# Moving a store's issue and the wait for a free output tile within one pipelined unit of a softmax-mixture kernel

## The chip, the cores and the metric

The kernel runs on one core of one Trainium2 chip; the metric is device microseconds of that core. A run counts as slow when it lies over 1.5% above the fastest run of the same kernel; slow runs are left out of the ratios.

## The reference

```python
# float32: logits (batch 32, seq 128, heads 4, vocab 4096), prior (32, 128, 4)
prior_probs = softmax(prior, axis=-1)
softmax     = softmax(logits, axis=-1)
mixture     = sum over heads of prior_probs[..., None] * softmax   # (32, 128, 4096)
```

268 MB come in, 67 MB go out, and each number is touched a few times: there is little arithmetic per byte.

## The kernel before

The 4096 rows are worked off in 32 units (U = 32) of 128 rows. The helper `only` replaces all inferred waits of an instruction by the ones named. `H` is the number of heads, 4; `bufd` is true for all units but the last two. A unit's logits go to one of two input tiles, its result to one of two output tiles (`obuf`).

```python
def load(u):                       # issued by SyncE, 8.39 MB; cut finer for u = 0 and u >= 29
    ...
    only(ld, adds[u - 2, 0] ...)   # the input tile is free when add0 two units back is done
def store(u, acc, eng):            # 2.10 MB
    st = eng.dma_start(out=ov[u // J, u % J], in_=acc)         # shortened
    stores[u] = only(st, adds[u, H - 1])                       # waits for the unit's last add
...
def exp(h, *keep):                 # ScalarE, 4096 columns, sum of the row in dsum
    ex = nc.scalar.activation(es[h], lt[:, h], AF.Exp, accum_out=dsum[:, u, h : h + 1])
    keep = (loads[u, h],) + keep
    if bufd and h and u:
        keep += (adds[u - 1, h],)
    exps[u, h] = only(ex, *keep)
def weigh(h, n, *keep):            # 1 / sum on VectorE, times prior on GpSimd
    rc = nc.vector.reciprocal(rden[:, u, h : h + n], dsum[:, u, h : h + n])
    only(rc, exps[u, h + n - 1])
    mul = nc.gpsimd.tensor_mul(coeff..., rden..., ppu...)      # shortened
    return only(mul, rc, *keep)
...
free = (stores[u - 2],) if bufd and u >= 2 else ()   # the output tile's last store
m = H if u < U - 4 else 2                            # one group of four heads, two of two at the end
for h in range(H):
    late = h == H - 1 and 4 <= u < U - 3
    if h == H - 1 and 0 < u < U - 3:
        store(u - 1, obuf[:, (u - 1) % 2], nc.scalar)          # issued by ScalarE
    exp(h, *((stores[u - 4],) if late else ()))
    if (h + 1) % m:
        continue
    g = h + 1 - m
    mul = weigh(g, m, *(free if g == 0 else ()))
    ...                                                        # add0 to add3 on VectorE
if u + 2 < U:
    load(u + 2)
```

I call the four exponentials of a unit exp0 to exp3 and its four multiply-adds add0 to add3. The output tile is first written by add0, which waits for the coefficient; so the wait for the tile may sit anywhere ahead of that.

The softmax here doesn't subtract the row's maximum and nothing guards it: scores larger than these inputs give would overflow.

## Time and profile before

| | kernel before |
|---|---|
| time, median of 6 runs | 780.94 us (780.90 to 781.00) |
| period of a unit in the middle | 24.17 us |
| load, issue to landing | 30.9 us |
| store, issue to landing | 29.4 us |
| ScalarE's wait for loads, sum | 280.6 us |

Most lines are shown in the prediction. Two more views help. The first is the page's chain of work that ended last, as shares of the span by engine:

```profile
DMA 64%; ACT 27%; DVE 6%; issue 2%; POOL 0%; DVEq 0%; POOLq 0%
```

Followed back from the end, most of the time is waiting for transfers. The second is the table of stretches; its columns are the stretch, its length, busy time of VectorE, ScalarE and GpSimd (with instructions), the clock, the share of time in which transfer engines are busy, and GB/s:

```profile
301.75:398.45 96.70, 63.94 (x21) 58.02 (x32) 0.80 (x4) 1.00 1.00 434
398.45:495.15 96.70, 63.94 (x21) 58.02 (x32) 0.81 (x4) 1.00 1.00 434
```

A stretch is four units. VectorE works 64 of 96.7 us, the transfers all of it.

### The profile page before, as it was taken

Reading aid. Unit: us, or ns where it says so; the run is one execution under the profiler, and the core shown is the slowest. Engines: PE = TensorE matmul, PEld = TensorE weight load, DVE = VectorE, ACT = ScalarE, POOL = GpSimd, SP = SyncE. Lnnn points to the kernel's source line nnn. Section 1 sums busy time; section 2 is a strip of 40 time slices with the busy share of each in tenths; the row PEclk is TensorE's granted clock in tenths of the full one; section 3 lists DMA queues with packets and bytes.
Section 4 is the critical chain, followed back from the end, with each engine's and each line's share of the span. In section 5 each row is a group of like instructions: output and inputs, shape, how many; then the busy total and the mean of one; then the engine's idle time right before and its main releaser. Section 6 shows DMA issues by size and latency. Waiting matters only on the chain.

```text
span 779.3 us, 654 instructions
## 1 busy us (share of the span) xinstructions
DVE 521.0 (67%) x174; ACT 466.7 (60%) x258; POOL 8.3 (1%) x41
## 2 busy tenths in 40 slices
DVE  4447875558755587555775557855578655689886
ACT  4476555775457755577555675546765567657782
POOL 0000000000000000000000000000000000000000
DMA  9999999999999999999999999999999999999998
GB/s 407 457 417 401 470 407 434 428 461 428 405 467 403 458 420 433 442 443 418 431 454 407 454 408 467 420 415 447 432 442 417 463 399 463 410 427 433 434 429 377
DMA packets 10117, 335.66 MB, mean 431 GB/s; under 512 B 1136, under 2 KB 1136, under 8 KB 1152
## 3 DMA queue, kind: packets, MB, share of 16 engines
q1 hardware_dynamic: 6048, 276.83, 82.3%
q10 hardware_dynamic: 4064, 58.79, 17.6%
q14 instruction: 5, 0.04, 0.0%
HBM read 268.50 MB, written 67.11 MB: 431 GB/s over the span
## 4 chain that ended last, share of the span: by engine, by line
DMA 64%; ACT 27%; DVE 6%; issue 2%; POOL 0%; DVEq 0%; POOLq 0%
DMA ltile<-in_logits_dram 62%; ACT ebuf L159 19%; ACT ltile L159 8%; DVE obuf L177 5%; DMA out_dram<-obuf 2%; DVE ltile L183 1%; POOL coeff L170 0%; DVE rden L168 0%; DVEq L240 0%; POOLq L240 0%; POOLq L170 0%
## 5 line engine op out<-in xcount | busy, mean ns | idle before, releaser
L183 DVE SCALAR_TENSOR_TENSOR obuf<-ebuf,coeff,obuf 128x4096 f32<-128x4096 f32 x90 | 403.6, 4484 | 3.8 <-POOL coeff L170 0.6
L159 ACT ACTIVATE ebuf<-ltile 128x4096 f32<-128x4096 f32 x90 | 322.9, 3589 | 7.4 <-DMA ltile<-in_logits_dram 7.4
L159 ACT ACTIVATE ltile<-ltile 128x4096 f32<-128x4096 f32 x38 | 137.3, 3614 | 280.6 <-DMA ltile<-in_logits_dram 280.6
L168 DVE RECIPROCAL rden<-dsum 128x4 f32<-128x4 f32 (+1 forms) x36 | 6.3, 175 | 227.9 <-ACT ebuf L159 225.1
L177 DVE TENSOR_SCALAR obuf<-ltile,coeff 128x4096 f32<-128x4096 f32 x30 | 70.6, 2353 | 10.2 <-POOL coeff L170 10.2
L183 DVE SCALAR_TENSOR_TENSOR ltile<-ltile,coeff 128x4096 f32<-128x4096 f32 (+1 forms) x7 | 27.0, 3875 | 0.8 <-POOL coeff L170 0.6
L159 ACT ACTIVATION_READ_ACCUMULATOR ebuf<-ltile 128x1 f32 x90 | 16.8, 186 | 0.0
L170 POOL TENSOR_TENSOR coeff<-rden,pp 128x4 f32<-128x4 f32 (+1 forms) x36 | 7.2, 200 | 755.3 <-DVE rden L168 745.4
L159 ACT ACTIVATION_READ_ACCUMULATOR ltile<-ltile 128x1 f32 x38 | 7.1, 186 | 0.0
L139 DVE TENSOR_REDUCE pmax<-pr 16x256 f32<-16x1024 f32 x1 | 1.2, 1208 | 7.8 <-DMA pr<-in_prior_dram 7.8
L141 ACT ACTIVATE pr<-pr 16x1024 f32<-16x1024 f32 x1 | 1.1, 1055 | 7.8 <-DVE pr L140 7.8
L177 DVE TENSOR_SCALAR ltile<-ltile,coeff 128x4096 f32<-128x4096 f32 x2 | 4.7, 2354 | 0.6 <-POOL coeff L170 0.6
L144 DVE TENSOR_TENSOR pn<-pr,pmax 16x1024 f32<-16x1024 f32 x1 | 1.9, 1939 | 0.1
L141 ACT ACT_TABLE_LOAD x1 | 1.3, 1283 | 1.2 <-PEq L229 1.2
L142 DVE TENSOR_REDUCE pmax<-pr 16x256 f32<-16x1024 f32 x1 | 1.2, 1207 | 1.1 <-ACT pr L141 1.1
L149 DVE STREAM_TRANSPOSE pp<-pn 32x256 f32<-32x256 f32 x4 | 1.7, 435 | 0.1
L143 DVE RECIPROCAL pmax<-pmax 16x256 f32<-16x256 f32 x1 | 1.7, 1741 | 0.0
L140 DVE TENSOR_TENSOR pr<-pr,pmax 16x1024 f32<-16x1024 f32 x1 | 1.2, 1211 | 0.0
L138 POOL MEMSET pn<- 32x1024 f32 x1 | 0.9, 941 | 0.3 <-POOLq L229 0.3
L229 POOL MEMSET const-bfloat16-1.0<- 128x1 bf16 x1 | 0.1, 106 | 0.0
L229 POOL MEMSET const-uint8-127<- 128x1 uint8 x1 | 0.1, 106 | 0.0
L229 POOL MEMSET const-float32-0.0<- 128x1 f32 x1 | 0.1, 103 | 0.2 <-issue 0.2
(1 smaller groups left out, 0.1 us busy)
## 6 DMA issues: line engine op xcount, KB each, us to landing
out_dram<-obuf ACTq DMA_DIRECT2D x28, 2048.0 KB, 29.4
ltile<-in_logits_dram SPq DMA_DIRECT2D x7, 4096.0 KB, 26.1
ltile<-in_logits_dram SPq DMA_DIRECT2D x2, 2048.0 KB, 30.9
out_dram<-obuf SPq DMA_DIRECT2D x2, 2048.0 KB, 33.9
out_dram<-ltile SPq DMA_DIRECT2D x1, 2048.0 KB, 17.2
out_dram<-ltile SPq DMA_DIRECT2D x2, 1024.0 KB, 4.8
ltile<-in_logits_dram SPq DMA_DIRECT2D x28, 30.9
pr<-in_prior_dram ACTq DMA_DIRECT2D x1, 64.0 KB, 7.0
```

Source lines behind the costliest of these rows:

```text
L139: nc.vector.reduce_max(pmax, pr, axis=AX.X)
L140: nc.vector.tensor_sub(pr, pr, pmax.unsqueeze(2).to_broadcast([G, R, H]))
L141: nc.scalar.activation(pr, pr, AF.Exp)
L142: nc.vector.reduce_sum(pmax, pr, axis=AX.X)
L143: nc.vector.reciprocal(pmax, pmax)
L144: nc.vector.tensor_mul(pn[0:G].rearrange("g h r -> g r h"), pr, pmax.unsqueeze(2).to_broadcast([G, R, H]))
L149: nc.vector.transpose(pp[32 * t : 32 * (t + 1)], pq[:, :, :, 32 * t : 32 * (t + 1)])
L159: ex = nc.scalar.activation(es[h], lt[:, h], AF.Exp, accum_out=dsum[:, u, h : h + 1])
L168: rc = nc.vector.reciprocal(rden[:, u, h : h + n], dsum[:, u, h : h + n])
L170: mul = nc.gpsimd.tensor_mul(coeff[:, u, h : h + n], rden[:, u, h : h + n], ppu[:, h : h + n])
L177: st = nc.vector.tensor_scalar(out=acc[:, lo:hi], in0=es[h][:, lo:hi], scalar1=coeff[:, u, h : h + 1], scalar2=None, op0=ALU.mult,)
L183: st = nc.vector.scalar_tensor_tensor(out=acc[:, lo:hi], in0=es[h][:, lo:hi], scalar=coeff[:, u, h : h + 1], in1=acc[:, lo:hi], op0=ALU.mu ...
```

## The change

The intent: get the store out sooner, and take the wait for the output tile off the short path from the last exponential to the first add, onto an engine that waits for loads anyway.

```diff
             for h in range(H):
-                late = h == H - 1 and 4 <= u < U - 3
-                if h == H - 1 and 0 < u < U - 3:
+                if h == 2 and 0 < u < U - 3:
                     store(u - 1, obuf[:, (u - 1) % 2], nc.scalar)
-                exp(h, *((stores[u - 4],) if late else ()))
+                exp(h, *(free if m == H and h == H - 1 else ()))
                 if (h + 1) % m:
                     continue
                 g = h + 1 - m
-                mul = weigh(g, m, *(free if g == 0 else ()))
+                mul = weigh(g, m, *(free if m < H and g == 0 else ()))
```

## The prediction

> **What bounds the kernel now.** I read the page first, then the transfer view of a steady stretch, then the waits, then the timeline of one unit. A unit is 128 rows: one 8.39 MB load, four exponentials (exp0 to exp3) on ScalarE, four multiply-adds (add0 to add3) on VectorE, one 2.10 MB store; there are 32. From the page:
>
> ```profile
> DVE 521.0 (67%) x174; ACT 466.7 (60%) x258; POOL 8.3 (1%) x41
> ...
> DMA  9999999999999999999999999999999999999998
> ...
> HBM read 268.50 MB, written 67.11 MB: 431 GB/s over the span
> ```
>
> No compute engine is above 67%, while the transfer engines are at 90% or more in 39 of 40 slices. Four units of the middle (400 to 496.7 us):
>
> ```profile
> DMA packets 1152, 41.94 MB, mean 434 GB/s; under 512 B 128, under 2 KB 128, under 8 KB 128
> ...
> q1 hardware_dynamic: 576, 33.55, 80.1%
> q10 hardware_dynamic: 576, 8.39, 20.3%
> ...
> out_dram<-obuf ACTq DMA_DIRECT2D x4, 2048.0 KB, 29.4
> ltile<-in_logits_dram SPq DMA_DIRECT2D x4, 30.9
> ```
>
> Loads (q1) and stores (q10) get the same number of packets, 576 each, and so bytes as 4 to 1, which is just what a unit needs. A load takes 30.9 us from issue to landing and a store 29.4, both longer than a unit's period of 24.17 us (96.7 / 4). So each queue gets its next transfer before its last has landed: neither runs dry. The rate table confirms it: six stretches of four units from 108 to 688 us all show 434 GB/s. Waits:
>
> ```profile
> POOL coeff L170 <- DVE rden L168: 745.4, 35, 28.3
> ACT ltile L159 <- DMA ltile<-in_logits_dram: 280.6, 32, 12.0
> ...
> POOL coeff L170 <- DMA out_dram<-obuf: 10.0, 1, 10.0
> ```
>
> ScalarE waits for loads in 32 units, 280.6 us in all. GpSimd, which today waits for the store two units back before the coefficient, is held by it once, in the tail; elsewhere it waits for VectorE's reciprocal. The wait that moves is free where it stands.
>
> **What the Trainium skill says.** "DMA: Bandwidth & Descriptors", section "Queues, rings and completion order": each transfer engine goes round-robin between its queues, a packet at a time. The 576 against 576 agree. The same page, section "Where 436 GB/s comes from", puts the fabric's ceiling at 435 GB/s; the 434 agrees. It also says that HBM at about 358 GB/s binds such transfers; this trace, one core alone, shows 434, and the measurement decides. "Perfetto Trace Analysis", section "Per-engine timelines": ScalarE's sequencer puts a compute instruction in a queue and goes on, but waits for a transfer's semaphores itself. Both show in unit 26:
>
> ```profile
> 645.09 3.62 ACT L159 ACTIVATE ltile<-ltile 128x4096 f32<-128x4096 f32 x1 [9.65 <-DMA ltile<-in_logits_dram]
> ...
> 648.71 3.60 ACT L159 ACTIVATE ebuf<-ltile 128x4096 f32<-128x4096 f32 x1
> 651.90 0.34 ACTq L113 DMA_DIRECT2D out_dram<-obuf  x1
> ...
> 652.31 3.56 ACT L159 ACTIVATE ebuf<-ltile 128x4096 f32<-128x4096 f32 x1
> ...
> 655.90 3.60 ACT L159 ACTIVATE ebuf<-ltile 128x4096 f32<-128x4096 f32 x1
> ...
> 659.63 0.18 DVE L168 RECIPROCAL rden<-dsum 128x4 f32<-128x4 f32 x1 [7.75 <-ACT ebuf L159]
> ...
> 662.51 4.48 DVE L183 SCALAR_TENSOR_TENSOR obuf<-ebuf,coeff,obuf 128x4096 f32<-128x4096 f32 x1
> ```
>
> The store's issue stands after exp2 in the program, yet goes out at 651.90, before exp2 starts at 652.31. What it waited for is add3 of the unit before, which ends at 638.35 + 13.53 = 651.88.
>
> **The change, part by part.** The order of VectorE's and SyncE's instructions and their waits is unchanged; ScalarE and GpSimd have as many instructions as before.
>
> 1. *The store's place.* 28 stores (0 to 27, each issued in the unit after its own) move one exponential forward. The gain is nothing: the issue is already held by add3 (0.02 us from 651.88 to 651.90), not by its place. The cost: exp2 now stands behind it. It can start at 651.88 + 0.02 + 0.34 (the issue) + 0.03. The last term is the gap at the start of the trace between the end of ScalarE's first transfer issue, 0.79 + 0.39 = 1.18, and the table load behind it at 1.21. That gives 652.27, against 652.31 today: in step by chance, no delay. This makes a new loop: add3, issue, exp2, exp3, reciprocal, coefficient, add0 to add3. From exp2's start to the end of add3 it is 662.51 + 13.52 - 652.31 = 23.72 us, and with the 0.39 it is 24.11, against the 24.17 at which the transfers let units through. If the gap is really 0.15, the loop is 24.23, and compute drifts back by 0.06 x 27 units = 1.6 us over the whole run.
>
> 2. *The wait.* GpSimd loses its wait for the store two units back in the four-wide units, 26 of its multiplications. exp3 trades its wait for the store four units back (from unit 4), long landed, for the store two units back. Store 24 goes out at 627.74 and takes 29.4, so it lands at 657.1; exp3 would start at 655.90 and now waits until 657.1, 1.2 us. GpSimd's multiplication at 659.88 found it landed. So a hidden wait becomes a visible one, in nearly every unit. It doesn't add up per unit, though: landings are 24.17 us apart, so exp3 is late by 1.2 us in every unit, once for all. Add3 then ends 676.03 - 655.90 = 20.13 us after the landing, and its store goes out 24.17 - 20.15 = 4.0 us before the store ahead of it lands. The store queue stays fed.
>
> 3. *What the delay does to loads.* The load two units ahead goes out when add0 ends. Today that is at 662.51, and the load in flight lands at 638.34 + 30.9 = 669.25: 6.7 us ahead. Later by 1.2 us it is 5.5 us ahead; with the drift of part 1 still 3.9. If the load queue did empty for a moment, the store queue would hold a store with over 13 us to go (it went out 10.6 us before the load's issue and needs 24 or more), and the engines would move that. Bytes only trade places; idle engines would need both queues empty at once.
>
> Sum for the steady part: 0 us, out of 1.2 to 2.8 us of later compute that lies beside transfers.
>
> 4. *Head and tail.* In unit 2, add3 of unit 1 ends at 59.15 + 13.53 = 72.68, later against the load than in the middle, so exp2 slips from 71.80 to about 73.1, and load 4 from 82.00 to 83.3, still 4.8 us before load 3 lands at 88.15. In the tail units 28 and 29 keep their wait on GpSimd, on stores 26 and 27. Store 27 goes out some 1.2 to 2.5 us later than 700.23, and the one visible GpSimd wait, which ends at 718.33, moves with it. That delays add0 and add1 of unit 29 (ending 725.53), but add2 starts only at 727.94, behind exp3 of that unit: up to 2.4 us are swallowed. Load 31's first part goes out with the end of that add0, at 721.03, and starts its first exponential at 749.22, with 28 us in between that are transfers queued ahead of it: hidden. Those bytes are the same, so the end stays, give or take half a microsecond.
>
> Predicted: 780.93 + 0 steady + about 0.1 for head and tail = 781.0 us.
>
> **The rivals.**
>
> *The new wait stalls ScalarE and is paid in each unit.* For it: exp3 visibly waits 1.2 us, and 1.2 x 26 = 31 us would make 812. Against: ScalarE is idle about 9.65 us in each unit before exp0, waiting for the load, and takes the 1.2 out of that; and landings keep a 24.17 us rhythm of their own.
>
> *The loop through the store's issue becomes the bound.* 24.11 is only 0.06 under the period. If the gap behind the issue is 0.5 us, the loop is 24.58, and in 27 units compute falls 0.41 x 27 = 11 us behind the loads. The first 5 are covered by the queue's lead, 6 come onto the time: 787 us. For a loss of 2% (15.6 us) the gap must be about (15.6 + 5) / 27 + 0.06 = 0.8 us; the one such gap in the trace is 0.03.
>
> *Earlier or better spaced stores help.* A stretch at 434 GB/s has nothing to give. All bytes at that rate take 335.6 MB / 434 = 773.3 us of 779.3; the 6 us of difference are the first transfer's start and the drain after the last add, which this doesn't touch. A gain of 2% is out of reach; at best the tail, at 420 GB/s over its last 91 us, gives 2 us: 779.
>
> **Range and chances.** The central case is no change; repeats of the kernel before lie within 0.1 us. Downward there are at most some 1.5 us of better mixing in the tail; upward the drift, up to about 3 us. Range 779.5 to 783.8. Faster by over 2%: 0.01; slower by over 2%: 0.03, nearly all of it the second rival; within 2%: 0.96.
>
> **What would show it.** Right: in the middle 434 GB/s, equal packets, period 24.17; a new wait of ScalarE for stores of 1 to 2 us in most units, its wait for loads smaller by as much; the store's issue again 0.02 us after add3, with exp2 right behind it; store latency down from 29.4 to about 28 us, and load latency from 30.9 to about 29.5; GpSimd's only wait for a store still in the tail. Wrong: a period above 24.2 with idle transfer slices (the loop bounds), a load landing late in unit 30 or 31, or a gap of over 0.5 us between the store's issue and exp2.

## The result, and the profile after

The changed kernel takes 780.98 us (median of 6 runs, 780.91 to 781.09), the kernel before 780.94 beside it. The ratio is 1.0001, with a 95% interval from 0.9988 to 1.0013. (A ratio is the mean time of one kernel's fast runs over that of the other's in the same rounds, so not quite the ratio of the medians.) The time is the same; the inside isn't. The transfers of four units in the middle (400 to 496.7 us) of the changed kernel:

```profile
DMA packets 1152, 41.94 MB, mean 434 GB/s; under 512 B 128, under 2 KB 128, under 8 KB 128
...
out_dram<-obuf ACTq DMA_DIRECT2D x4, 2048.0 KB, 28.0
ltile<-in_logits_dram SPq DMA_DIRECT2D x4, 29.5
```

The bytes and the rate are those of before. Both latencies are 1.4 us shorter: each transfer is issued later and lands when it did. Its waits (who for whom, sum in us, times, longest):

```profile
ACT ltile L159 <- DMA ltile<-in_logits_dram: 241.5, 32, 12.0
...
ACT ebuf L159 <- DVE obuf L183: 36.0, 26, 2.1
...
POOL coeff L170 <- DMA out_dram<-obuf: 10.7, 1, 10.7
```

The new line is the middle one: 26 times, 36.0 us in all, an exponential waits for an add. ScalarE's wait for loads fell by 39.1 us from 280.6, so the new wait was taken out of the old one. There is no line in which ScalarE waits for a store. The same unit as in the prediction, in the timeline (start, length, engine, line; in brackets the engine's idle time before the instruction and what ended it; ACTq is ScalarE's sequencer, which issues the stores):

```profile
645.01 3.62 ACT L159 ACTIVATE ltile<-ltile 128x4096 f32<-128x4096 f32 x1 [8.38 <-DMA ltile<-in_logits_dram]
...
653.10 0.34 ACTq L113 DMA_DIRECT2D out_dram<-obuf  x1
653.49 3.59 ACT L159 ACTIVATE ebuf<-ltile 128x4096 f32<-128x4096 f32 x1 [1.17 <-DVE obuf L183]
657.10 3.60 ACT L159 ACTIVATE ebuf<-ltile 128x4096 f32<-128x4096 f32 x1
...
663.71 4.49 DVE L183 SCALAR_TENSOR_TENSOR obuf<-ebuf,coeff,obuf 128x4096 f32<-128x4096 f32 x1
```

exp2 starts at 653.49 instead of 652.31, 0.05 us behind the end of the store's issue at 653.44; exp3 follows with no gap, and add1 starts 1.20 us later than before. The load lands as before (645.01 against 645.09). The chain that ended last has turned over:

```profile
DVE 55%; ACT 26%; DMA 15%; issue 2%; ACTq 1%; POOL 1%; DVEq 0%; SPq 0%; POOLq 0%
```

Read alone, this says that VectorE and ScalarE bound the changed kernel. It takes experiments to tell whether they do: the chain picks at each step what came last, and here two things come at nearly the same time.

### The profile page after: what moved, and what is told of

The parts are those of the page before. It is cut to its first block, busy times and chain, and to the rows that moved or that the text cites. A ratio compares the mean times of both kernels' runs of the same rounds, so it can differ in the third digit from the quotient of the medians.

```text
span 779.2 us, 628 instructions
## 1 busy us (share of the span) xinstructions
DVE 521.0 (67%) x174; ACT 469.8 (60%) x258; POOL 8.4 (1%) x41
## 4 chain that ended last, share of the span: by engine, by line
DVE 55%; ACT 26%; DMA 15%; issue 2%; ACTq 1%; POOL 1%; DVEq 0%; SPq 0%; POOLq 0%
DVE obuf L183 45%; ACT ebuf L159 24%; DMA ltile<-in_logits_dram 9%; DVE obuf L177 8%; DMA out_dram<-obuf 6%; ACT ltile L159 1%; ACTq L113 1%; DVE ltile L183 1%; POOL coeff L170 1%; DVE rden L168 1%; DVEq L241 0%; SPq L100 0%; POOLq L241 0%; POOLq L170 0%
## 6 DMA issues: line engine op xcount, KB each, us to landing
ltile<-in_logits_dram SPq DMA_DIRECT2D x7, 4096.0 KB, 25.5
ltile<-in_logits_dram SPq DMA_DIRECT2D x28, 29.5
```

## The experiments

The theory: the transfers set 24.17 us per unit, and the change only uses up idle time of compute. Rivals: the two halves of the change cancel; the compute loop (last add, store's issue, exp2, exp3, reciprocal, coefficient, add0 to add3) is the new bound; each transfer queue must always be fed. Three groups each shared a chip and their runs of the kernel before: place_only, wait_only, store_before_exp1 and pad_half; short_add1, pad_two, before_pad_two and wait_on_exp0; wait_on_exp2 and wait_on_exp1. All were timed in three rounds. All results are correct but for one.

**place_only: the store's place alone.**

```diff
-                if h == H - 1 and 0 < u < U - 3:
+                if h == 2 and 0 < u < U - 3:      # everything else as before
```

> Only the store's issue moves ahead of the third exponential; the waits stay as in the kernel before. Theory (transfers set the period of 24.17 us, compute lies beside them): 781.0 us, and the third exponential (exp2) waits 1.2 to 1.8 us for the last add of the unit before, as in the changed kernel, while nothing waits for a store's landing on ScalarE. Rival (the two halves of the change cancel, one slower, one faster): this one is off by more than 2 us, and the run with the wait alone by as much the other way.

Measured: 781.03 us beside 781.00, ratio 1.0001 (0.9984 to 1.0018). Latencies in the middle are 27.8 (store) and 29.3 us (load), and the wait of exp2 is there:

```profile
ACT ebuf L159 <- DVE obuf L183: 39.6, 26, 2.4
```

So the place alone makes the whole delay. As in the changed kernel it starts in unit 2, where add3 of unit 1 ends late against the load, and then it stays. In the changed kernel the wait is 1.26 us in unit 2, 1.84 in unit 3 and still 1.17 in unit 26: the loop takes as long as the period to within 0.03 us, so what is lost once is hardly won back.

**wait_only: the wait alone.**

```diff
-                exp(h, *((stores[u - 4],) if late else ()))
+                exp(h, *(free if m == H and h == H - 1 else ()))
...
-                mul = weigh(g, m, *(free if g == 0 else ()))
+                mul = weigh(g, m, *(free if m < H and g == 0 else ()))
```

> Only the wait moves from GpSimd to the fourth exponential (exp3); the store stays ahead of exp3. Theory: 781.0 us; exp3 of most units is seen to wait about 1.2 us for the landing of the store two units back, the store's latency falls from 29.4 to about 28 us and the load's from 30.9 to about 29.5. Rival (in the changed kernel only the store's place made the delay, and the wait for the landing holds nothing): latencies stay at 29.4 and 30.9.

Measured: 781.10 us beside 781.00, ratio 1.0002 (0.9987 to 1.0016); latencies 28.1 and 29.6 us. The wait for the landing shows, 26 times 1.13 us:

```profile
ACT ebuf L159 <- DMA out_dram<-obuf: 29.3, 26, 1.4
```

In its timeline it stands ahead of exp3:

```profile
608.93 3.62 ACT L159 ACTIVATE ebuf<-ltile 128x4096 f32<-128x4096 f32 x1 [1.16 <-DMA out_dram<-obuf]
```

So each half by itself delays the adds by about 1.2 us, and the two don't add: where exp2 is already 1.2 us late, exp3 finds the store landed. In the changed kernel the first half hides the second. Neither moves the time by more than the intervals leave open, under 1.5 us, so no two effects of 2 us or more cancel.

**short_add1: less VectorE work in the loop.** As the changed kernel; add1 works on half its columns (relative error 0.27). Its output is wrong, which doesn't matter for the time.

```diff
+                    if bufd and h == 1:
+                        hi = lo + 2048
                     st = nc.vector.scalar_tensor_tensor(
```

> As the changed kernel, but the second multiply-add works on half its columns (wrong result on purpose), about 2.2 us less VectorE time in the loop. Theory (the transfers bound): 781.0 us, VectorE busy time down by about 67 us, exp2 no longer waits for the last add, and exp3 is now seen to wait about 1.2 us for the store's landing. Rival (the compute loop, which the chain of waits of the changed kernel now runs through, has become the bound): faster, up to 2 us per unit or 50 us.

Measured: 781.07 us beside 780.93, ratio 1.0002 (0.9988 to 1.0017). Busy times on its page, and its wait for loads:

```profile
DVE 457.1 (59%) x174; ACT 466.7 (60%) x258; POOL 8.4 (1%) x41
```

```profile
ACT ltile L159 <- DMA ltile<-in_logits_dram: 281.2, 32, 12.0
```

VectorE works 64 us less, the wait of exp2 is gone, ScalarE again waits 281 us for loads, and the time stays. This settles what the chain left open: the compute loop doesn't bound the changed kernel, though it fills the period. (No run moved fewer bytes; that the transfers do bound rests on the rate, 434 GB/s before and after, and on less compute gaining nothing.) One part of the expectation missed: no wait of exp3 for a store appears. With shorter adds the stores go out sooner and land sooner: the one that exp3 of 608.02 us needs, issued one period before the store of 601.87, at 577.7, lands after 28.5 us, at 606.2.

**pad_half: half a microsecond more in the loop.** A dummy activation on a scratch tile, between the store's issue and exp2.

```diff
+        pz = nc.gpsimd.memset(padi, 0.0)            # padi, pado: 128 x 470
...
+                if h == 2 and 0 < u < U - 3:
+                    only(nc.scalar.activation(pado, padi, AF.Exp), pz)
                 exp(h, *(free if m == H and h == H - 1 else ()))
```

> As the changed kernel, with a dummy activation of about 0.48 us between the store's issue and exp2, inside the loop. Theory (the loop of 24.17 us equals the period, and the transfers outstanding at a load's issue, about 6 us of work, are the only cushion): 26 x 0.48 - 6 = 6.5 us slower, 787.5 us (784 to 792). Rival A (loop has slack left): 781. Rival B (no cushion): 793.5.

Measured: 791.22 us beside 781.00, ratio 1.0131 (1.0116 to 1.0146): clear of the noise. Two successive store issues of the timeline are 24.65 us apart:

```profile
615.36 0.34 ACTq L113 DMA_DIRECT2D out_dram<-obuf  x1
615.75 0.59 ACT L201 ACTIVATE pado<-padi 128x470 f32<-128x470 f32 x1 [4.10 <-DVE obuf L186]
616.25 3.57 ACT L162 ACTIVATE ebuf<-ltile 128x4096 f32<-128x4096 f32 x1
...
640.01 0.34 ACTq L113 DMA_DIRECT2D out_dram<-obuf  x1
```

The period grew by the 0.48 that was put in: the loop of the changed kernel has no slack. The last of these stores goes out at 714.0 instead of 701.4 us, 12.6 later, which is 26 x 0.48; the time grew by 10.2. So 2.4 us were covered, not the 6 that I had estimated. How the profile shows a loss of 1.3% is worth a look; the page's slices, in tenths, and then the table of stretches say:

```profile
DMA  9999999999999999999999999999999999999998
```

```profile
398.45:495.15 96.70, 63.94 (x20) 58.52 (x35) 0.80 (x4) 1.00 1.00 426
```

The transfer engines read as busy all the time, as before (1.00 ahead of the last number). Only the rate, 426 instead of 434 GB/s, tells that they don't bound any more.

**pad_two: two such dummies.** The dummy's line stands there twice.

> As the changed kernel with two dummy activations of about 0.48 us each in the loop. Theory (cushion of about 6 us once, then each added us of the loop is paid in each of 26 units): 26 x 0.96 - 6 = 19 us slower, 800 us (796 to 804), so 12.5 us above the run with one. Rival A (slack left in the loop): under 790. Rival B (no cushion): 806.

Measured: 809.15 us (807.08 to 809.64) beside 780.93, ratio 1.0356 (1.0340 to 1.0371). That is 9 us over the expectation. Two reasons make 6.5 of it. The second dummy costs 0.63 us, not 0.48: the period is 25.28 (604.57 to 629.85), 1.11 over 24.17, and 26 x 1.11 = 28.9. And again little is covered: the last store goes out 29.5 us later than in the changed kernel (730.9 against 701.4), the profiled span is 26.1 us longer (805.3 against 779.2), so 3.4 us. The profiled run was also the fastest of the four, 2.1 us under the median.

**before_pad_two: the same two dummies in the kernel before.**

```diff
+                if h == 2 and 0 < u < U - 3:
+                    only(nc.scalar.activation(pado, padi, AF.Exp), pz)
+                    only(nc.scalar.activation(pado, padi, AF.Exp), pz)
                 exp(h, *((stores[u - 4],) if late else ()))
```

> The kernel before with the same two dummy activations ahead of exp2, where no store's issue stands behind them in the loop. Its loop through the store's issue and exp3 is about 20.5 us, 3.6 under the period. Theory: 781.0 us, ScalarE waits about 1 us less for each load. Rival (the dummies cost their time anywhere): 800 us.

Measured: 781.52 us beside 780.93, ratio 1.0008 (0.9993 to 1.0023). The same 1.11 us per unit that cost 28 us in the changed kernel costs 0.6 us in all here, within the interval. ScalarE waits less for loads (280.6 us without the dummies):

```profile
ACT ltile L162 <- DMA ltile<-in_logits_dram: 250.2, 32, 12.0
```

The kernel before has over 1 us of slack in each unit, the changed kernel none.

**store_before_exp1: the store one exponential further forward.**

```diff
-                if h == 2 and 0 < u < U - 3:       # the changed kernel
+                if h == 1 and 0 < u < U - 3:
```

> As the changed kernel, with the store ahead of the second exponential: the loop last add, issue, exponentials, coefficient, adds becomes 24.17 + 3.61 = 27.8 us, over the period of the transfers. Theory (the loop is real and only fits under the period by chance): 26 units times 3.6 us and 1.2 us at the start, less about 6 us of outstanding transfers that run on meanwhile: 870 us (862 to 878), DMA about 88%. Rival (the sequencer runs ahead enough that the place of the issue never holds an exponential): 781 us.

Measured: 874.22 us beside 781.00, ratio 1.1194 (1.1177 to 1.1211). The rate in the middle fell to 380 GB/s. The exponential behind the issue waits 13 us in each unit, for the add:

```profile
601.49 0.34 ACTq L113 DMA_DIRECT2D out_dram<-obuf  x1
601.88 3.62 ACT L159 ACTIVATE ebuf<-ltile 128x4096 f32<-128x4096 f32 x1 [13.13 <-DVE obuf L183]
...
629.26 0.34 ACTq L113 DMA_DIRECT2D out_dram<-obuf  x1
```

The period is 27.77 us, the loop with one more exponential, as worked out. It confirms that the issue holds all of ScalarE's work behind it, whatever is ready.

**wait_on_exp0, wait_on_exp2, wait_on_exp1: the wait for the store further forward.** The store's issue stands ahead of exp3, as in the kernel before and in wait_only; only the exponential that waits for the landing is another (k = 0, 2, 1). wait_on_exp0 ran first.

```diff
-                exp(h, *(free if m == H and h == H - 1 else ()))   # wait_only
+                exp(h, *(free if m == H and h == k else ()))
```

> The wait for the store two units back sits on the first exponential of a unit, the store's issue ahead of exp3 as in the kernel before. The next store then goes out about 7 us after the store ahead of it has landed, so the store queue is empty for a part of each unit. Theory (only both queues empty at once costs time; when one is empty the other moves its bytes): 781 us, within 3; a store then takes some 17 us instead of 29. Rival (each queue must stay fed): a store needs 24 us beside loads, the loop over two units is 31 + 24 = 55 us instead of 48.3, 14% or about 90 us slower.

Measured: 886.51 us (885.51 to 889.23) beside 780.93, ratio 1.1363 (1.1344 to 1.1382). My theory fell here, by 105 us: I had argued that bytes only trade places while one of the queues has work; the rival, with a loop of 55 us over two units and about 90 us lost, came near. The loop in the timeline, from a landing to the issue of the unit's own store 31.0 us later and to that store's landing after another 23.6:

```profile
585.03 3.62 ACT L159 ACTIVATE ltile<-ltile 128x4096 f32<-128x4096 f32 x1 [22.10 <-DMA out_dram<-obuf]
...
616.00 0.34 ACTq L113 DMA_DIRECT2D out_dram<-obuf  x1
...
639.66 3.62 ACT L159 ACTIVATE ltile<-ltile 128x4096 f32<-128x4096 f32 x1 [19.57 <-DMA out_dram<-obuf]
```

The late wait also holds up add0 and with it the next load, and so both queues do run empty at once: the last load has landed at 593.4 us, the store of 585.20 at 597.1, and the next load goes out at 602.4; between 598 and 602 us the trace shows 0 GB/s. I mended the theory and tried the two places between.

> The wait for the store two units back sits on the third exponential (exp2), the store's issue ahead of exp3. From that landing to the end of the last add it is then 23.7 us, so the next store goes out 0.4 us before the store ahead of it lands. Theory as mended after the run with the wait on exp0 (no loss as long as the next store is issued before the one ahead has landed, because then the wait repeats with the landings' own 24.17 us): 781 to 784 us, load lead down to about 2 us. Rival (any step of the wait towards the front costs its 3.6 us or a share of it in each unit): above 800 us.

Measured: 810.62 us (806.07 to 818.50) beside 780.93; the three fast runs have a median of 808.85 and a ratio of 1.0339 (1.0318 to 1.0360). The mended theory fell too.

> The same wait on exp1: landing to the end of the last add is 27.4 us, so the store goes out 3.2 us after the one ahead has landed. Mended theory: the two-unit loop is 27.4 + 24 to 26 us of store beside loads, 25.7 to 26.7 us a unit, 821 to 847 us. Rival (only both queues empty at once costs, and here they need not be): 781 us.

Measured: 844.92 us (838.57 to 846.83) beside 780.93, ratio 1.0804 (1.0759 to 1.0850); this one came out as the mended theory had it. The timeline of wait_on_exp2 shows what I had left out:

```profile
611.24 3.59 ACT L159 ACTIVATE ebuf<-ltile 128x4096 f32<-128x4096 f32 x1 [8.39 <-DMA out_dram<-obuf]
611.29 0.34 ACTq L113 DMA_DIRECT2D out_dram<-obuf  x1
...
635.02 0.34 ACTq L113 DMA_DIRECT2D out_dram<-obuf  x1
...
661.07 3.59 ACT L159 ACTIVATE ebuf<-ltile 128x4096 f32<-128x4096 f32 x1 [8.42 <-DMA out_dram<-obuf]
```

The store of 611.29 lands after 12.0 us, that of 635.02 after 26.0, and so on in turn: the loop closes over two units. From exp2 of a unit to the issue of that unit's own store 23.8 us pass (635.02), its landing takes 26.0, and exp2 of the unit two further on starts: 49.8 us from 611.24 to 661.07, against two periods, 48.3. A neighbouring pair takes 50.7 (the stores of 560.6 and 611.3). Thirteen pairs (26 units) with an excess of 1.5 to 2.4 us make 20 to 31 us; the profiled run, at 812.39, is 31 us over. The term that I got wrong is the store's latency when its queue starts out empty: 26 us beside a running load, not what is left of a period. (The stores that an exponential waits for take 23.6 to 30.1 us in the three runs, on average 26.9 with the wait on exp2, 26.4 on exp1 and 25.5 on exp0.) With 26 us the row comes out, each step forward adding 3.6 us to the way from landing to the last add:

| wait for the store on | landing to last add, plus 26 us of store | against 48.3 us | time |
|---|---|---|---|
| GpSimd (before) | 16.2 + 26 = 42.2 | under | 780.9 |
| exp3 (wait_only, changed kernel) | 20.1 + 26 = 46.1 | under by 2.2 | 781.1, 781.0 |
| exp2 | 23.8 + 26 = 49.8 | over by 1.5 | 808.9 (fast runs) |
| exp1 | 27.4 + 26 = 53.4 | over by 5.1 | 844.9 |
| exp0 | 31.0 + 26 = 57.0 | over by 8.7 | 886.5 |

Thirteen times the excess is 20, 66 and 113 us; measured are 28, 64 and 106. So the loop's sum fits all five places. It was worked out after these runs, and no further run tested it; nor do they part it from the rule that the store queue must stay fed, for in wait_on_exp2 that queue too stood empty, from 623.3 us to 635.0. No version tried is faster than the kernel before.

## Why the prediction was right or wrong

The time was right to 0.02 us (781.0 predicted, 780.98 measured), and the reason held: the rate in the middle is 434 GB/s with and without the change, short_add1 shows that less compute gives nothing, and place_only and wait_only show that neither half costs or gains. (The equal packet counts are no sign of how the queues take turns: each unit needs 144 packets of either queue, so any steady state gives 576 against 576.) The latencies came as predicted, 28.0 for about 28 and 29.5 for about 29.5, but by another way: the delay that shortened them sits at exp2, not at exp3. The tail came as predicted too: GpSimd's multiplication behind its wait for store 27 starts at 720.27 instead of 718.42, later by 1.9 us, and add2 of unit 29 starts at 727.85 against 727.94. So what was wrong lies in the steps.

*Part 1, "in step by chance, no delay".* Wrong. exp2 is late by 1.2 us in the unit shown of the changed kernel, and it is the wait that the profile shows, 36.0 us in 26 units. I had computed that step from a unit of the kernel before, as if it started fresh; part 4 had the 1.3 us of unit 2, but not that a loop as long as the period carries them on. The loop measures 24.17 (653.10 to 677.27, issue to issue) against my 24.11: the gap behind the issue is 0.05 us instead of 0.03, and exp2 to the last add takes 23.75 instead of 23.72.

*Part 2, exp3's visible wait.* Right in size only where the wait moves alone (1.13 us each, wait_only). In the changed kernel it never shows, since part 1's delay comes first. One delay was predicted, one was measured; it sits one exponential earlier.

*Part 3, "Bytes only trade places".* Right for this change, wrong as a rule. It would have made wait_on_exp0 free, which costs 106 us. What failed there is the premise that one of the two queues always has work; both stand empty for about 5 us in the pair of units looked at. In the two pairs of wait_on_exp2 looked at, some transfer is in flight all the time, by issue and landing, and still they are 1.5 and 2.4 us longer; where the engines lose that, the runs don't show. By the table's sum the loop over two units has about 2 us to spare here, which I had not worked out. That is an estimate: the 26 us in it vary by more, and no run tested it.

*The second rival, and the range.* The loop did come to the very edge: 24.17 on 24.17, without the 0.06 that I had left. That the time stayed is luck to this extent: 0.48 us more per unit, and it is 10 us longer. The size of the fall behind the edge was too small: for 0.5 us more I had 787, with 5 us covered first; 0.48 more gave 791.2, with 2.4 covered. The slower side of the range was too short for the risk that it named, had the gap been larger than 0.05.

## What to carry to other kernels

When transfers bound a kernel, the place of a wait is free, as far as these runs go, until the loop that it closes is as long as the transfers' period: add up each loop, over as many units as there are buffers, with the transfer's own latency in it, and compare with the period. A change that leaves the time alone may still have used up all the slack; a dummy of known length put into the loop measures that at once (1.11 us per unit here: 0.6 us in the kernel before, 28 us in the changed one). Read the rate and not the busy share: transfer engines that no longer bound still showed as fully busy.

## What the Trainium skill lacked or had wrong

- "DMA: Bandwidth & Descriptors", section "Where 436 GB/s comes from", lets HBM bind loads and stores at about 358 GB/s, though it names a measurement of 425 GB/s beside it. One core alone moved 434 GB/s in the steady part of both kernels.
- The same page, section "Queues, rings and completion order", describes the turns of the queues, but no page says what a transfer's latency becomes by it. Here the same 2.1 MB store took 12.0 us, 26.0 or 29.4, as the load queue was empty for part of it, was busy, or the store also stood behind another. Loops through a landing need that number.
- "Perfetto Trace Analysis" gives the order of a transfer's issue and the compute instructions behind it, without times. Here a store's issue occupied ScalarE's sequencer for 0.34 us, and the exponential behind it started 0.05 us later.
